# Output projection of a hybrid layer as seven products of block sums through DRAM, with the second norm's transposes set among the up projection's first products

## The chip, the cores and the metric

One core of one Trainium2 chip. The core has engines with a queue each: TensorE (matmul, and its weight load beside it), VectorE, ScalarE, GpSimd, and SyncE, which in this kernel issues all transfers between DRAM and the on-chip memory, one after the other in the order of its queue. An engine takes its instructions in order; one that waits for another engine holds up all that stand behind it.

The metric is the device time of one execution in microseconds, as a median of runs. Beside it there is a hardware profile of one execution, whose span goes from its first to its last instruction.

## The reference

One layer over 1024 tokens of width D = 1024, cut to what matters here (the inner width F of the feed-forward part is 2816):

```python
hx = modulate(rmsnorm(x), sh1, sc1)                  # (T, D)
q, k, v, rq, rk, rv, rg, ga, gb = split(hx @ w_in)
o_na  = neighbourhood_attention(q, k, v, ctx)        # (T, 512)
o_ret = two_way_retention(rq, rk, rv, ctx) * silu(rg)  # (T, 1024)

merged = sigmoid(ga) * (o_na @ w_proj_na) + sigmoid(gb) * (o_ret @ w_proj_ret)
x   = x + g1 * (merged @ w_out)                      # output projection, gated residual
hx2 = modulate(rmsnorm(x), sh2, sc2)                 # second norm
u   = conv3_over_tokens(hx2 @ w_up)                  # (T, 2F), three taps and a bias
a, val = split(u)
x   = x + g2 * ((silu(a) * val) @ w_down)
return rmsnorm(x, final_gain)
```

All inputs and the output are float32.

## The kernel before, in words

**Products.** Each float32 operand is split in a high part (ScalarE copies it to the rounded form, L86) and a low part (VectorE subtracts the copy from the original, L87), and each product is three matmuls: high x high, high x low, low x high. A matmul is 128 x 128 weights against 128 x 512 moving elements. Activations lie in two layouts: channels on the partitions and tokens along the row (128 channels x 512 tokens, a half of the tokens), or tokens on the partitions (a token block is 128 tokens).

**Seven products.** Where the text says "seven products of block sums", a product of 2 x 2 blocks is computed with seven block products in place of eight (the Winograd form): four sums S1 to S4 of the left blocks A11 to A22, four sums T1 to T4 of the right blocks B11 to B22, then A11 B11, S2 T2, A12 B21, S3 T3, S1 T1, A22 T4, S4 B22, whose results are added up. The kernel before does this for the gates, for the up projection (class `Seven`, its subclass `Up`) and for the down projection (`steps`), but not for the output projection. The sums of the down projection's weights (`down_sums`, GpSimd, L1249) are made in three earlier stages and kept in DRAM (`d_w`); its activations' sums go through DRAM too (`d_a`).

**Order.** A scheduler puts the instructions of most stages in the engines' queues by priority and estimated time; what is wrapped in `late(...)`, and the stages under a manual schedule, keep the order of the program. All transfers stand on SyncE's queue.

**The stages around the change.**
- *Merge* (L1588 to L1624, some 87 us): for each of eight blocks `db` of 128 channels and two halves of the tokens, `pret` computes the retention projection in 24 matmuls (`pr`, L110 to L112), VectorE multiplies it by the gate (L1592), GpSimd adds the attention part that waits in DRAM (L1593; VectorE for the last block), and the sum is split into high and low parts that stay on the chip. Blocks run in order 0 to 7. Each block needs two weight tiles (`pret_load`, from `in_w_pret`) and four tiles of gates and attention parts (`merge_load`, from `d_gate` and `d_pn`). Beside them `out_sums` makes the last of the sums for `d_w`, one step per half.
- *Output projection* (`out_proj`, L1631 to L1658, some 95 us): all of `w_out` is on the chip, split. For each of eight token blocks and two halves of D, 24 matmuls (`om`, L121 to L123) give 128 tokens x 512; VectorE multiplies by the gate row `gate1` and adds `x`. The row's mean square goes to ScalarE, then the power of -1/2 to GpSimd.
- *Second norm* (`norm_out`, L1660 to L1692): one token block behind the projection, eight transposes on TensorE (L1671) give channels on the partitions; ScalarE writes the high part with gain and shift (L1677), VectorE the full value (L1679) and the low part (L1680), 128 x 128 each. The values of the first four token blocks go to DRAM (`d_h`); with those of the other four they make the T sums for the up projection's seven products (four VectorE subtractions of 128 x 512 per token block, `d_t`).
- *Up projection, first two column blocks* (`up`, L1701; loop L1838): plain products of 4 x 48 matmuls (24 per branch and half of the tokens), into double banks of PSUM (`u`, 128 x 1024). The first half of both branches of the first block (`early`, L1712) runs between the last projection and the last transposes. After each pair a convolution over the tokens (`conv`, L1754) reads PSUM. Between the pairs `comb` (L1780) loads and splits the T sums, four tiles of 128 x 512 for each of T1 to T4.
- *Up projection, the other 20 column blocks*: units `Up` (L1789, L1848), each seven products of four k-blocks x 3 = 84 matmuls, the weights' sums made by GpSimd (L1380 to L1383).

## Time and profile before

| | |
|---|---|
| device time, median of 3 runs | 1765.64 us (1763.32 to 1767.51) |
| profiled execution, span from first to last instruction | 1759.2 us; what lies around the span is not recorded apart |
| mean granted TensorE clock of the profiled execution | 0.996 |
| TensorE matmul, busy | 1726.0 us (98%), 8405 instructions |
| VectorE, busy | 1284.2 us (73%) |
| ScalarE, busy | 849.2 us (48%) |
| GpSimd, busy | 539.3 us (31%) |
| moved by transfers | 261.10 MB |
| merge stage, 920.5 to 1007.6 | GpSimd busy 29.92 of 87.10 us |

How to read the rows of the profile: a group row has the line of the program, engine, operation, output <- inputs by their names in the program, partitions x elements, the count, then busy time and mean duration of one (ns), then idle time of the engine just before them and what ended it. A row of a stretch (first to last time) has for PE, PEld, DVE (VectorE), ACT (ScalarE) and POOL (GpSimd) the busy time and count, then TensorE's granted clock (1.00 is full), the share of the transfer engines, and GB/s. Rows of waits name the engine that waited, for which tile, and who released it: sum, count and longest. SPq is SyncE's queue. Rows of transfers have the KB of one and the time from issue to landing.

### The profile page before, as it was taken

To read this page: it belongs to the slowest core of one execution; us is meant where nothing else is said; L and a number is where in the kernel's file an instruction comes from. 1 tells how busy PE (TensorE), PEld (TensorE's weight loads), DVE (VectorE), ACT (ScalarE), POOL (GpSimd) and SP (SyncE) were. 2 spreads that over 40 slices of the span, in tenths; PEclk is the share of its full clock that TensorE was granted. 3 is DMA by queue.
4 is the path that set the end of the run, shared out by engine and by line. 5 is a ranking of instruction groups with operands and counts; after the bars stand their busy time and mean duration, and the time that the engine had idled before them with its cause. 6 is when DMAs were issued, how large, how long until landed. Compare 5 with 4: busy or idle time off the path is not lost.

```text
span 1759.2 us, 24801 instructions
## 1 busy us (share of the span) xinstructions
PE 1726.0 (98%) x8405; PEld 1429.3 (81%) x8405; DVE 1284.2 (73%) x2454; ACT 849.2 (48%) x1826; POOL 539.3 (31%) x455
## 2 busy tenths in 40 slices
PE   8999999999999999999999999989999999999997
PEld 4688988888888888778888888778888888788886
DVE  4778887756776766777665557868899889875755
ACT  5666666653443434443444324534444444554444
POOL 1000000003334343555413300165555655211444
PEclk9999999999999999999999999999999999999999
DMA  9143334342231212677557733733322332586754
GB/s 348 61 130 125 95 117 147 117 133 87 73 108 43 72 42 68 203 238 239 200 199 268 246 143 132 254 108 102 108 90 92 118 120 90 170 296 192 239 162 162
DMA packets 139408, 261.10 MB, mean 148 GB/s; under 512 B 15856, under 2 KB 28304, under 8 KB 139280
## 3 DMA queue, kind: packets, MB, share of 16 engines
q1 hardware_dynamic: 139280, 259.51, 44.3%
q8 instruction: 66, 1.08, 0.3%
q14 instruction: 62, 0.51, 0.1%
HBM read 187.34 MB, written 69.48 MB: 146 GB/s over the span
## 4 chain that ended last, share of the span: by engine, by line
PE 43%; issue 6%; DVE 4%; POOL 3%; DMA 1%; ACT 1%; SPq 0%; POOLq 0%; ACTq 0%; DVEq 0%
PE u L1374 30%; PE y L1374 4%; PE pr L112 2%; PE pr L111 2%; PE pr L110 2%; PE om L122 1%; PE om L121 1%; PE om L123 1%; POOL x L1902 1%; DVE wc L87 0%; DVE b L1350 0%; DVE v L1679 0%; POOL pd L1939 0%; DVE hxT L87 0%; POOL x L1947 0%
## 5 line engine op out<-in xcount | busy, mean ns | idle before, releaser
L1374 PE MATMUL u<-T,wc 128*128 128x512 f32 x960 | 227.1, 392 | 5.1 <-ACT pu L1408 5.1
L1374 PEld LDWEIGHTS u<-T,wc 128*128 128x128 f32 x960 | 180.6, 189 | 45.7 <-ACT pu L1408 7.9
L1374 PE MATMUL y<-wc,ahl 128*128 128x512 f32 x924 | 210.6, 389 | 2.7 <-DVE wc L87 1.8
L1374 PEld LDWEIGHTS y<-wc,ahl 128*128 128x128 f32 x924 | 173.3, 188 | 39.7 <-DVE wc L87 2.5
L87 DVE TENSOR_TENSOR wc<-ur,wc 128x512 fp32r<-128x512 f32 x137 | 122.7, 897 | 65.8 <-ACT wc L86 65.8
L86 ACT CAST wc<-ur 128x512 fp32r<-128x512 f32 x137 | 85.0, 621 | 129.7 <-PE y L1374 72.3
L111 PE MATMUL mm<-low,wc 128*128 128x512 f32 (+1 forms) x328 | 124.0, 378 | 0.0
L1374 PE MATMUL u<-h2a,wc 128*128 128x512 f32 x480 | 112.3, 389 | 0.7 <-DVE pu L1417 0.7
L110 PE MATMUL mm<-hx,wc 128*128 128x512 f32 x264 | 107.4, 407 | 0.2 <-ACT wc L589 0.2
L1374 PEld LDWEIGHTS u<-h2a,wc 128*128 128x128 f32 x480 | 90.0, 188 | 19.8 <-DVE pu L1417 1.2
L112 PE MATMUL mm<-hx,wc 128*128 128x512 f32 x264 | 105.2, 399 | 0.0
L86 ACT CAST wc<-s 128x512 fp32r<-128x512 f32 x80 | 49.7, 623 | 93.2 <-PE u L1374 88.3
L123 PE MATMUL mm<-wc,low 128*128 128x512 f32 (+1 forms) x240 | 91.2, 380 | 0.0
L1374 PE MATMUL u<-hxT,wc 128*128 128x512 f32 x384 | 89.6, 389 | 0.0
L1508 POOL TENSOR_TENSOR col<-col,bcol 128x32 f32<-128x32 f32 x1 | 0.3, 253 | 280.7 <-DVE aw L538 280.7
L87 DVE TENSOR_TENSOR wc<-s,wc 128x512 fp32r<-128x512 f32 x80 | 83.5, 1046 | 3.8 <-ACT wc L86 3.4
L1374 PEld LDWEIGHTS u<-hxT,wc 128*128 128x128 f32 x384 | 72.1, 188 | 14.9
L87 DVE TENSOR_TENSOR wc<-raw,wc 128x512 fp32r<-128x512 f32 x92 | 68.0, 746 | 17.7 <-ACT wc L86 17.7
L121 PE MATMUL mm<-wc,hx 128*128 128x512 f32 x192 | 75.2, 392 | 0.6 <-ACT r L1105 0.6
L122 PE MATMUL mm<-wc,hx 128*128 128x512 f32 x192 | 75.2, 392 | 0.0
L1383 POOL TENSOR_TENSOR s<-ur 128x512 f32<-128x512 f32 x20 | 35.7, 1783 | 126.3 <-DVE wc L87 68.7
L86 ACT CAST wc<-raw 128x512 fp32r<-128x512 f32 x92 | 56.8, 621 | 33.0 <-PE pr L112 6.0
(393 smaller groups left out, 4671.3 us busy)
## 6 DMA issues: line engine op xcount, KB each, us to landing
ur<-in_w_up SPq DMA_DIRECT2D x80, 256.0 KB, 2.9
ur<-d_a SPq DMA_DIRECT2D x77, 256.0 KB, 3.1
aw<-in_w_ada SPq DMA_DIRECT2D x32, 512.0 KB, 3.3
pj<-in_w_down SPq DMA_DIRECT2D x44, 256.0 KB, 5.2
d_w<-pj SPq DMA_DIRECT2D x44, 256.0 KB, 2.0
d_a<-sa SPq DMA_DIRECT2D x44, 256.0 KB, 2.0
ur<-d_w SPq DMA_DIRECT2D x44, 256.0 KB, 3.8
d_a<-at SPq DMA_DIRECT2D x33, 256.0 KB, 2.7
```

Source lines behind the costliest of these rows:

```text
L86: act.copy(hi, src)
L87: (lo_eng or vec).tensor_tensor(lo, src, hi.bitcast(F32), ALU.subtract)
L110: pe.matmul(out, wh, xh, start=k == 0, stop=False)
L111: pe.matmul(out, wh, xl, start=False, stop=False)
L112: pe.matmul(out, wl, xh, start=False, stop=k == n - 1)
L121: pe.matmul(out, ah, bh, start=first, stop=False)
L122: pe.matmul(out, ah, bl, start=False, stop=False)
L123: pe.matmul(out, al, bh, start=False, stop=last)
L1374: pe.matmul(out, a, b, start=first and n == 0, stop=last and n == 2, skip_group_check=True)
L1383: pool.tensor_tensor(self.s1, self.a21, self.a22, ALU.add)
L1508: pool.tensor_tensor(col[:, 16:48], col[:, 16:48], bcol[:, 16:48], ALU.add)
L1902: pool.tensor_tensor(z, z, fg[:, gs(dh)], ALU.mult)
```

## The change

- **Output projection as seven products.** Left operands are blocks of the merged activations: A11, A12, A22 are stored by `pret` itself, S1 to S4 are made by VectorE (`mg_sums`, after both blocks j and j + 4 are there), all into `d_m`. Right operands are made by GpSimd (`out_sums`): it multiplies `w_out` by the gate row `gate1` and makes T1 to T4, all into `d_wo`, 3 steps per half of a merge block. Merge blocks run in the order 0, 4, 1, 5, 2, 6, 3, 7. `pret` no longer splits its result. A `Stream` loads the operands from DRAM eight ahead (10 buffers), and `out_ops` splits both per product and k-block.
- **Accumulation.** Products lie in two sets of four PSUM banks, one bank per token block; results are combined on VectorE (`p1`, `u2`, `u3`), and GpSimd adds `x` in half rows. `out_last` finishes a token block's row norm.
- **The norm turned per four token blocks.** `turn2` transposes one channel block of four token blocks into one bank and evicts 128 x 512 at a time; the turns of half 1 stand beside the last product and the first plain up products, those of half 0 beside the next. Plain up products go channel block by channel block over two (column blocks) x two (branches) accumulators. The weights `wu[0]` are loaded and split a second time for the last quarter.
- **T sums** are made by GpSimd per channel block (`token_sums`), in place of VectorE per token block; `d_h` is gone.
- **PSUM** of the up projection is eight single banks; the first two column blocks are copied to `uu` by ScalarE ahead of their convolution.
- **`w_down` sums** are all made before the merge stage: one step in two of the gates stage in place of one in three.

The core of the diff:

```diff
-    RET_SUMS, GATE_SUMS = 5, 9
+    RET_SUMS = 5
...
-        if n % 3 == 1:
+        if n % 2:
             next(gate_sums, None)
...
+    def out_sums():
...
+        for j in range(KH):
+            nxt = []
+            for n, (t, c) in enumerate(zip(ts, ("B11", None, "B21", "B22"))):
+                late(pool.tensor_tensor(t, t, gate1[:, n % 2 * 512 : n % 2 * 512 + 512], ALU.mult))
+                if c:
+                    sync.dma_start(d_wo[j, BLOCKS[c]], t)
+                if j + 1 < KH:
+                    nxt.append(load(j + 1, n))
+                yield
+            b11, b12, b21, b22 = ts
+            t1, t2, t4 = (tile_() for _ in range(3))
+            for c, o, x, y in (("T1", t1, b12, b11), ("T3", b12, b22, b12), ("T2", t2, b22, t1), ("T4", t4, b21, t2)):
+                late(pool.tensor_tensor(o, x, y, ALU.subtract))
+                sync.dma_start(d_wo[j, BLOCKS[c]], o)
+                yield
+            ts = nxt
...
     def pret(db, half):
...
-        g = sg[db, 1, half]
+        mg[db, half] = g = sg[db, 1, half]
         vec.tensor_tensor(g, m, g, ALU.mult)
         (vec if db == KB - 1 else pool).tensor_tensor(g, g, sg[db, 0, half], ALU.add)
-        h_, l_ = gtile(half, F32R, "mh"), gtile(half, F32R, "ml")
-        split(h_, l_, g)
-        mg[db, half] = (h_, l_)
+        if (db // KH, half) != (0, 1):
+            sync.dma_start(d_m[{(0, 0): A11, (1, 0): A12, (1, 1): A22}[db // KH, half], db % KH], g)
+
+    def mg_sums(j):
+        a11, a21, a12, a22 = (mg[j + KH * i, half] for i in range(2) for half in range(2))
+        s1, s2, s3, s4 = (gtile(n % 2, F32, "s") for n in range(4))
+        for c, o, x, y, op_ in ((S1, s1, a21, a22, ALU.add), (S2, s2, s1, a11, ALU.subtract), (S3, s3, a11, a21, ALU.subtract), (S4, s4, a12, s2, ALU.subtract)):
+            vec.tensor_tensor(o, x, y, op_)
+            sync.dma_start(d_m[c, j], o)
...
+    dbs = [db for j in range(KH) for db in (j, j + KH)]
...
+    mg_sums(0)
+    ostream = Stream([(j, c) for p in ORDER for j in range(KH) for c in p], 8, out_source, xr_load)
-    for db in range(2, KB):
+    for n, db in enumerate(dbs[2:]):
         wp[db] = pret_load(db)
         merge_load(db)
-        if db == 2:
-            brow(0, gate1)
         for half in range(2):
             pret(db, half)
-            next(out_sums, None)
+            for _ in range(3):
+                next(out_sums, None)
+        if db >= KH:
+            mg_sums(db - KH)
+    for _ in out_sums:
+        pass
...
+    def out_ops(p, js):
+        tl = []
+        for j in js:
+            a, w = (gtile(1, F32R, "ah"), gtile(1, F32R, "al")), wtile()
+            split(*a, ostream.get((j, ORDER[p][0])))
+            split(w[:, 0], w[:, 1], ostream.get((j, ORDER[p][1])))
+            tl.append((j, a, w))
+        return tl
...
+    def out_last(tb, dh, p, x):
+        z[tb, dh] = t = t_tile("z")
+        vec.tensor_tensor(t, bank(p % 2, tb % QB), x, ALU.add)
+        out_square(tb, dh)
+        s = ss[:, tb]
+        pool.tensor_scalar(s[:, 3:4], s[:, dh : dh + 1], 1.0 / D, s[:, 2:3], ALU.mult, ALU.add)
+        pool.tensor_tensor(s[:, 4:5], s[:, 3:4], mhalf[:, 0:1], ALU.pow)
+        for d in (1 - dh, dh):
+            xn[tb, d] = t_tile("xn")
+            act.activation(xn[tb, d], z[tb, d], AF.Copy, scale=s[:, 4:5])
...
+    def turn2(half, kb, tp):
...
+        for b in range(QB):
+            pe.transpose(tp[:, b * P : (b + 1) * P], xn[half * QB + b, kb // KH][:, kb % KH * P : (kb % KH + 1) * P], ident)
...
+        act.activation(h_, tp, AF.Identity, bias=sh, scale=a)
+        v2[half, kb] = v = t_tile("v")
+        vec.tensor_scalar(v, tp, a, sh, ALU.mult, ALU.add)
+        vec.tensor_tensor(l_, v, h_.bitcast(F32), ALU.subtract)
+
+    def token_sums(k):
+        b11, b21, b12, b22 = v2[0, k], v2[0, k + KH], v2[1, k], v2[1, k + KH]
+        for c, o, x, y in ((0, b11, b12, b11), (2, b12, b22, b12), (1, b22, b22, b11), (3, b21, b21, b22)):
+            pool.tensor_tensor(o, x, y, ALU.subtract)
+            sync.dma_start(d_t[c, k], o)
...
+    out_steps(0, True, False)
+    for b in range(QB):
+        p1[b] = t_tile("p1")
+        act.copy(p1[b], bank(0, b))
...
+    out_steps(5, False, True, 2)
+    tl = out_ops(5, (2, 3))
+    t7 = out_ops(6, (0, 1))
+    for b in range(QB):
+        out_mm(5, b, tl, False, True)
+        if b == 1:
+            t7 += out_ops(6, (2, 3))
+        out_last(QB + b, 0, 5, p1[b])
+
+    for n in range(2):
+        for b in range(QB):
+            out_mm(6, b, t7[n : n + 1], False, True)
+    tl = t7[2:]
+    for b in range(QB):
+        turn2(1, KORD[b], bank(1, 2 + b % 2))
+        out_mm(6, b, tl, False, True)
+        out_last(b, 1, 6, u2[b])
...
+    for n, k in enumerate(KORD):
+        if n + QB < KB:
+            turn2(1, KORD[n + QB], bank(1, 2 + n % 2))
+        for br in range(2):
+            up_k(us4[br], wu[0][br], 1, k, n)
+    for n, k in enumerate(KORD):
+        turn2(0, k, bank(0, n % 2))
+        if k >= KH:
+            token_sums(k - KH)
+        for br in range(2):
+            up_k(us4[2 + br], wu[1][br], 1, k, n)
+    for n, k in enumerate(KORD):
+        for br in range(2):
+            up_k(us4[2 + br], wu[1][br], 0, k, n)
+    wu[0] = [up_load(seq[1], br) for br in range(2)]
+    for n, k in enumerate(KORD):
+        for br in range(2):
+            up_k(us4[br], wu[0][br], 0, k, n)
...
-    for n, j in enumerate(seq[:PLAIN]):
-        us2 = []
-        for br in range(2):
-            u, wu = (u_tile(2 * n + br), up_load(j, br)) if n else early[br]
-            for half in range(2) if n else (1,):
-                up(u, wu, half)
-            us2.append(u)
+    for n in range(PLAIN):
         for c in ((1, 0), (2, 3))[n]:
             combs[f"T{c + 1}"] = comb(c)
-        conv(j, *us2)
+        uu = [tap.tile([P, T], F32, tag="uu", bufs=4, name="uu") for _ in range(2)]
+        for br in range(2):
+            for half in range(2):
+                act.copy(uu[br][:, half * 512 : half * 512 + 512], us4[2 - 2 * n + br][half])
+        conv(seq[n], *uu)
```

## The prediction

> **What bounds the kernel now.** I read the page first, then the busy time by stretch, the waits of TensorE and of the DMA queue, and last the rows of the stage that changes.

> ```profile
> span 1759.2 us, 24801 instructions
> PE 1726.0 (98%) x8405; PEld 1429.3 (81%) x8405; DVE 1284.2 (73%) x2454; ACT 849.2 (48%) x1826; POOL 539.3 (31%) x455
> ```
> ```profile
> 920.50:1007.60 87.10, 87.10 (x386) 72.13 (x385) 46.34 (x67) 35.16 (x60) 29.92 (x22) 1.00 0.76 258
> 1007.60:1102.30 94.70, 94.70 (x445) 78.60 (x444) 62.08 (x155) 31.82 (x70) 3.83 (x7) 1.00 0.40 148
> ```
> ```profile
> L110 PE MATMUL pr<-orr,wc x128: 389/389/389, 920.8 to 1007.2; 128*128 128x512 f32 x128
> L112 PE MATMUL pr<-orr,wc x128: 389/389/389, 921.3 to 1007.6; 128*128 128x512 f32 x128
> ```

> TensorE is busy 98% of the span, and in the two stretches that change (merge products to 1007.6, output projection to 1102.3) all of the time, at clock 1.00. So each matmul taken out is a gain at its pitch, each new wait of TensorE a loss in full. The pitch is not the 389 ns of a record: 384 matmuls start between 920.8 and 1007.6, so 0.2266 us each.

> ```profile
> PE u L1374 <- ACT pu L1408: 5.1, 1, 5.1
> PE tpn L1366 <- DVE ona L1369: 3.3, 1, 3.3
> PE u L111 <- DVE h2l L1680: 0.6, 2, 0.3
> ```
> ```profile
> 719.80:723.00 3.20, 3.17 (x12) 2.87 (x13) 3.20 (x6) 3.15 (x7) 3.20 (x4) 0.50 0.68 250
> 1156.50:1160.00 3.50, 3.43 (x8) 2.75 (x9) 3.50 (x5) 0.53 (x2) 0.74 (x1) 0.52 0.56 148
> ```

> The only waits near the change are 5.1 us, in the first seven-product unit of the up projection, and 0.6. The first two rows show a second price: after each of these waits (they end at 719.8 and 1156.5) the granted clock is 0.50 and 0.52 for 3.2 to 3.5 us. A wait of 3.3 us or more thus costs some 1.6 us on top.

> **The gain.** Seven products of 4 k-blocks by 4 token blocks by 3 passes are 336 matmuls in place of 384. 48 x 0.2266 = 10.9 us. The 64 transposes and the 192 plain up matmuls stay. Splits (ScalarE cast, VectorE remainder) go from 32 to 56, evictions grow to 128x512: both engines are under 70% busy here, so this costs nothing by itself. What decides is the order of the queues, which I took from the changed kernel as built: each engine takes its instructions in that order, and SyncE issues every DMA.

> **First wait: weights of merge block 3.** The merge products run over blocks 0, 4, 1, 5, 2, 6, 3, 7, two halves of 24 matmuls (5.44 us) each. The two weight loads of block 3 stand on SyncE behind the stores of block 6's sums:

> ```
> d_wo<-T1, d_wo<-T3, d_wo<-T2   of w_out block 2   [each waits GpSimd]
> d_m<-S1, d_m<-S2, d_m<-S3, d_m<-S4   of merge blocks 2, 6   [wait VectorE]
> raw<-in_w_pret, raw<-in_w_pret   for merge block 3
> ```

> S1 needs the last product of block 6, and TensorE has nothing to run between block 6 and block 3. In the kernel before these loads stood ahead of all such stores. That SyncE really stands still for such a store is seen here:

> ```profile
> 996.90 1.30 POOL L1249 TENSOR_TENSOR pj<-pj 128x512 f32<-128x512 f32 x1
> ```
> ```profile
> 998.23 0.33 SPq L1257 DMA_DIRECT2D d_w<-pj  x1
> 998.61 0.43 SPq L1571 DMA_DIRECT2D sg<-d_pn  x1
> ...
> SPq L1251 <- POOL pj L1249: 17.3, 7, 4.6
> ```

> The sum ends at 998.2, the store goes out at 998.23, and the load behind it only then; seven such stores held the queue 17.3 us, which hid behind loads made earlier. Prices:

> ```profile
> L1593 POOL TENSOR_TENSOR sg<-sg x14: 1277/1294/1674, 929.1 to 1000.7; 128x512 f32<-128x512 f32 x14
> ...
> L1249 POOL TENSOR_TENSOR pj<-pj x8: 1282/1292/1302, 956.1 to 996.9; 128x512 f32<-128x512 f32 x8
> ```
> ```profile
> L1592 DVE TENSOR_TENSOR sg<-pr,sg 128x512 f32<-128x512 f32 x15 | 10.3, 686 | 5.5 <-PE pr L112 5.0 <-ACT sg L1575 0.5
> L87 DVE TENSOR_TENSOR wc<-raw,wc 128x512 fp32r<-128x512 f32 x16 | 11.2, 703 | 2.8 <-ACT wc L86 2.8
> L86 ACT CAST wc<-raw 128x512 fp32r<-128x512 f32 x16 | 9.7, 620 | 9.3 <-PE pr L112 6.0 <-DMA raw<-in_w_pret 1.7 <-PE u L1374 1.4
> L1575 ACT ACTIVATE sg<-sg 128x512 f32<-128x512 f32 x8 | 5.1, 632 | 10.0 <-DMA sg<-d_gate 10.0
> ```
> ```profile
> raw<-in_w_pret SPq DMA_DIRECT2D x16, 256.0 KB, 3.5
> sg<-d_gate SPq DMA_DIRECT2D x16, 256.0 KB, 4.0
> ur<-d_t SPq DMA_DIRECT2D x16, 256.0 KB, 4.9
> d_t<-vo SPq DMA_DIRECT2D x8, 256.0 KB, 2.0
> ...
> 943.53 1.66 POOL L1593 TENSOR_TENSOR sg<-sg 128x512 f32<-128x512 f32 x1 [3.23 <-DVE sg L1592]
> ```

> Least case, GpSimd otherwise idle: block 6 ends at 12 x 5.44 = 65.3 (counted from 920.8). Product 0.69, sum on GpSimd 1.29, three w_out sums queued behind it 3.9, four stores of 0.33 each 1.3, load 2.9 to 3.5, cast 0.62: TensorE goes on at 76, a wait of 11. But GpSimd is not idle. Its queue holds, from the add of block 1 to those three sums, 8 merge adds and 23 w_out operations: 31 x 1.29 = 40 us. The fourth add ended at 945.2, that is 24.4. The four VectorE sums behind it and a split (5 x 0.69) end at 27.8; their stores head the gate loads of block 1, which land 4 us later, then sigmoid 0.63 and product 0.69: that add starts at 33. The gate loads of block 2 stand behind a w_out store in the same way, and GpSimd waits about 6 us for them. 33 + 40 + 6 = 79; stores, load and cast 5.4: TensorE starts block 3 near 85, a wait of 20. With the contended 1.67 in place of 1.29 it passes 25; I bound it at 11 and 23, since VectorE is idle while TensorE waits.

> [...]

> **Second wait: first output product.** Its third matmul needs the low part of A11, which stands on VectorE behind, for merge block 7: product, add, a split for product two, three sums, another split, the fourth sum. With its own subtraction 9 x 0.69 = 6.2 after the last merge matmul, less two matmuls 0.45: 5.7 at least (5.3 with 0.65 each). The splits ahead also wait for loads that SyncE issues after the last w_out store. I take 7, and 9 at most.

> **Inside the seven products** I charge nothing: operands are fetched eight ahead, and a product of 48 matmuls (10.9) covers eight casts (5.0) and eight subtractions with four evictions (8.3). Without that cover each product would cost the difference, and with GpSimd alongside VectorE it is thin.

> **Third: the turn.** Products five and six end in a row norm of four token blocks, then transposes that need all four.

> ```profile
> L1897 ACT ACTIVATE xr<-z 128x512 f32<-128x512 f32 x8 | 5.0, 628 | 14.9 <-DVE z L1972 8.9 <-POOL z L1958 6.0
> L1897 ACT ACTIVATION_READ_ACCUMULATOR xr<-z 128x1 f32 x8 | 1.5, 186 | 0.0
> L1906 POOL TENSOR_SCALAR ssf<-ssf 128x1 f32<-128x1 f32 x8 | 3.0, 381 | 16.3 <-ACT xr L1897 16.3
> L1907 POOL TENSOR_TENSOR ssf<-ssf,mhalf 128x1 f32<-128x1 f32 x8 | 4.7, 586 | 0.5
> L1909 ACT ACTIVATE x<-x,ssf 128x512 f32<-128x512 f32 x8 | 5.7, 717 | 5.6 <-POOL ssf L1907 5.6
> ```

> A token block takes ScalarE 0.63 + 0.19, then GpSimd 0.38 + 0.59 while ScalarE waits or casts a weight (0.62), then two scaled copies, 1.4: up to 3.4 us, four of them 13.7, against 9.5 of matmuls that TensorE has until then. Later the up matmuls wait several times under 2 us on VectorE, which evicts, scales and subtracts. I take 4; nothing, if casts and norms interleave better, to 8.

> **Fourth: T operands before weights.** The weights of the second value block of the up projection (wu[0], br 1) are cast on ScalarE behind the four casts of one T operand, and these need all sixteen token sums on GpSimd (16 x 1.29 = 20.6; 22.9 at 1.43), a store 2.0 partly beside, and the last d_t load. TensorE has six steps of 1.76 (six matmuls, four transposes), 47 matmuls and 3 more, 21.9, from about 1 us after the first sum starts. Sums end at 21 from there, issue 1.3, load 3 to 4.9, two casts 1.2: 27. Wait 5; between 0 and 9.

> **Fifth: copies before the first unit.** The plain up products now lie in eight single banks. For the second pair ScalarE makes four copies out of PSUM and two activations before it casts the first seven-product unit's weight; VectorE does four convolution steps before its low part.

> ```profile
> L1819 ACT COPY uu<-u 128x512 f32<-128x512 f32 x20 | 11.8, 588 | 3.1 <-PE u L1374 1.9
> L1759 ACT ACTIVATE ta<-uu,cb,cw 128x1024 f32<-128x1024 f32 x20 | 24.9, 1246 | 10.3 <-DVE uu L1398 9.9
> ...
> L1760 DVE SCALAR_TENSOR_TENSOR ta<-u,cw,ta 128x1023 f32<-128x1023 f32 x2 | 2.6, 1278 | 1.4 <-ACT ta L1759 1.4
> L1763 DVE TENSOR_TENSOR at<-ta,at 128x1024 f32<-128x1024 f32 x2 | 2.4, 1214 | 0.0
> ```

> 4 x 0.59 + 1.25 = 3.6, four steps of 1.28, 0.69, a product 1.21 and 0.69: 11.3, of which TensorE works 2.7. At least 8.5 against the 5.1 that stands there now: +3.4. As the T casts come late too, I take +5, up to 9.

> The gate stage gets eight more GpSimd sums (8 x 1.29) and their DMAs on SyncE; GpSimd was 40 to 55% busy there on the page, so I charge nothing.

> **Sum.** -10.9 + 20 + 7 + 4 + 5 + 5 = +30.1. Three of the waits are new ones over 3.3 us (first, second, fourth): 3 x 1.6 = 4.8. Together +34.9. Against the profiled span 1759.2 that is 1794. The median of the runs shown, 1765.64, is 6.4 above the span, and I keep that distance: 1800.5, rounded to 1800. The smallest price of each (11, 5.3, 0, 0, 3, clock 3.2) gives +11.6, 1777; the largest (23, 9, 8, 9, 9, clock 6.4) gives +53.5, 1819.

> **Rivals.**
> *Faster: the loads win.* If block 3's weights and A11 land before TensorE needs them, and the 5.1 us wait goes as well, the time is 1765.6 - 10.9 - 5.1 = 1749.6, 1750. It decides where SyncE reaches those two loads before 980 of the old trace, 6 us before block 3's turn. For it: stores held SyncE 17.3 us before and TensorE never waited. Against: a store ahead of the loads needs a product of block 6 itself. 7%.
> *Only the least chains bind.* GpSimd keeps up, and each wait is at its floor: the 1777 above, 1774 without its clock term. Against it are 31 operations behind an add that cannot start before 33. 20%.
> *The waits just eat the gain,* two of them missing: 1766. 4%.
> *GpSimd is the bound throughout.* With VectorE beside it at 1.67 (the slow records of the merge adds), first and fourth wait grow by 12 and 6: 1818, and with the fifth at its 9 as well 1822. 14%.
> *That the change does not do what it says* I rule out for the count: 336 products stand in the built order.
> The forecast holds 55%.

> A measurement of this kernel tells about 0.2% (3.5 us) from no change. Faster 0.07, same 0.04, slower 0.89. Range 1774 to 1822: the first and third rival lie below it, and little above.

> **What would show it.** In the profile after: a wait of TensorE of 11 us or more at the merge product that starts block 3, released by the cast of its weight, with SyncE issuing that load just after stores of d_wo and d_m; a second of 6 to 9 us at the first output product, released by VectorE; output products otherwise without a gap, 336 of them; GpSimd above 60% busy in the merge stage against 34% now; waits at the last plain up products and at the first unit; clock near 0.5 after each long one. I am wrong if block 3's weights are fetched ahead, if TensorE's waits between 920 and 1180 sum to less than 16 us, or if the seven products themselves starve, which I priced at nothing.

## The result, and the profile after

The changed kernel takes 1826.51 us (median of 4 runs, 1825.42 to 1828.57), the kernel before 1765.49 us beside it (1763.32 to 1767.51): a ratio of 1.035, 95% interval 1.0335 to 1.0365. The forecast was slower by 34.5 us (1800, range 1774 to 1822); it is slower by 61.0. The sign and the places of the waits held, the size did not.

The page's head, and TensorE's waits by what they waited for and who released them (sum, count, longest):

```profile
span 1823.6 us, 25072 instructions
PE 1731.4 (95%) x8357; PEld 1430.1 (78%) x8357; DVE 1314.0 (72%) x2362; ACT 865.0 (47%) x1850; POOL 634.8 (35%) x531
```
```profile
PE pr L111 <- ACT wc L87: 28.6, 1, 28.6
PE u L1734 <- ACT ah L87: 9.3, 1, 9.3
PE u L1734 <- ACT wc L87: 7.4, 3, 5.4
PE u L1778 <- ACT xn L1767: 6.3, 7, 3.2
PE u L122 <- ACT wc L87: 6.1, 1, 6.1
...
PE u L1734 <- DVE pu L1412: 2.6, 1, 2.6
PE u L1734 <- DVE wc L88: 2.6, 1, 2.6
...
PE u L1778 <- DVE v L1784: 1.5, 1, 1.5
```

The span grew by 64.4 us, from 1759.2 to 1823.6, and TensorE's share fell from 98% to 95%. The first five rows are the five places that the prediction named, in another order: the weights of merge block 3 (28.6), the first output product (9.3), the first units (7.4, with 2.6 and 2.6 below), the turn (6.3 and 1.5), the reloaded weights of branch 1 (6.1). Two stretches, the merge and the output products up to the first turn:

```profile
922.10:1040.60 118.50, 89.94 (x385) 73.77 (x384) 43.99 (x53) 19.76 (x32) 60.84 (x46) 0.87 0.79 277
1050.20:1127.60 77.40, 74.36 (x314) 60.45 (x314) 57.11 (x75) 42.05 (x84) 23.47 (x26) 0.96 0.76 260
```

GpSimd went from 34% to 51% of the merge stage, not over 60% as forecast; transfers stand at 79% and 76% of their engines' time, against 76% and 40% before.

**How the first wait came about.** SyncE's queue, then VectorE, GpSimd, ScalarE and TensorE, in order of time (start, duration; in brackets idle time before and its releaser):

```profile
998.17 0.32 SPq L1632 DMA_DIRECT2D d_wo<-pj  x1
999.02 0.45 SPq L1572 DMA_DIRECT2D sg<-d_pn  x1
999.51 0.43 SPq L1574 DMA_DIRECT2D sg<-d_gate  x1
...
1002.91 0.69 DVE L1651 TENSOR_TENSOR sg<-pr,sg 128x512 f32<-128x512 f32 x1 [11.40 <-DMA sg<-d_gate]
...
1003.73 1.26 POOL L1652 TENSOR_TENSOR sg<-sg 128x512 f32<-128x512 f32 x1 [0.71 <-DVE sg L1651]
1004.95 4.60 POOL L1639 TENSOR_TENSOR pj<-pj 128x512 f32<-128x512 f32 x3
...
1006.24 3.65 SPq L1640 DMA_DIRECT2D d_wo<-pj  x3
1009.99 1.97 SPq L1661 DMA_DIRECT2D d_m<-s  x4
1012.05 1.29 SPq L92 DMA_DIRECT2D raw<-in_w_pret  x2
...
1015.47 0.62 ACT L87 CAST wc<-raw 128x512 fp32r<-128x512 f32 x1 [25.96 <-DMA raw<-in_w_pret]
...
1016.14 0.79 PE L111 MATMUL pr<-orr,wc 128*128 128x512 f32 x1 [28.55 <-ACT wc L87]
```

The last merge product before the wait ended at 987.6. The gates that it is multiplied by were only asked for at 999.0, behind a store of `d_wo` whose sum GpSimd finished at 998.1. So VectorE multiplied at 1002.9 after 11.4 us idle, and GpSimd added at 1003.7. GpSimd's next three sums of `w_out` ended at 1009.6; their stores held SyncE until 1009.9, the merge sums were stored from 1010.0, and behind those stores, at 1012.05, stands the load of block 3's weights. It lands, is cast at 1015.47, and TensorE goes on at 1016.1.

**The clock.** The stretches in which the granted clock was low, or just after:

```profile
991.30:1016.10 24.80, 0.00 (x0) 0.00 (x0) 6.66 (x6) 0.62 (x1) 17.30 (x14) 0.50 0.75 270
1016.10:1021.90 5.80, 5.76 (x14) 4.46 (x15) 1.58 (x3) 2.69 (x5) 0.00 (x0) 0.50 0.98 349
1021.90:1027.00 5.10, 5.10 (x24) 4.22 (x23) 2.48 (x4) 1.06 (x2) 1.57 (x2) 0.99 0.64 244
1050.20:1055.90 5.70, 5.47 (x12) 3.92 (x13) 5.01 (x9) 3.10 (x6) 0.00 (x0) 0.50 0.94 302
1127.60:1131.00 3.40, 2.90 (x8) 2.21 (x9) 0.69 (x1) 2.87 (x6) 0.82 (x2) 0.53 0.69 191
1185.80:1192.50 6.70, 3.93 (x9) 3.03 (x10) 5.65 (x9) 5.97 (x12) 0.00 (x0) 0.50 1.02 339
1206.20:1219.80 13.60, 8.87 (x18) 5.65 (x19) 13.60 (x8) 3.94 (x7) 12.76 (x7) 0.51 0.16 59
1226.80:1230.10 3.30, 2.78 (x7) 2.21 (x8) 2.14 (x3) 0.00 (x0) 0.99 (x1) 0.50 0.45 112
```

Behind the wait of 28.6 the clock stays at 0.50 for 5.8 us (to 1021.9), behind that of 9.3 for 5.7, and at the units, where three short waits follow one of 5.4, for 13.6 us, of which TensorE is busy 8.9. Busy time at half clock sums to 5.76 + 5.47 + 2.90 + 3.93 + 8.87 + 2.78 = 29.7 us, about half of it lost (the records of merge matmuls go from 0.39 to 0.79 us there): 14.9. Before it was 1.7 in these stages.

The clock of this trace changes on a raster. Read in windows of 0.5 us, it drops at 991.3, 1045.9, 1127.8, 1185.9, 1206.3 and 1226.8 and comes back at 1022.0, 1056.1, 1131.2, 1192.7, 1220.0 and 1230.2, and all these times lie whole multiples of 3.41 us apart. So each slow stretch of this trace lasts a whole number of steps, its idle time included (9, 3, 1, 2, 4 and 1). Of the step in which the wait of 28.6 ends 2.5 us are work, and the clock stayed low for the next step too; of the step in which the turn's wait of 3.2 ends 3.1 us are work, and the clock came back at its end. In the row of short waits at the units it took four steps. Three waits end 0.9 (those of 28.6 and 9.3) and 2.7 us (the one before 1188.6) into a step: 5.8, 5.7 and 4.1 us of slow work follow, to the end of the next step. Two end 0.3 (the turn's) and 0.5 us (the one before 1227.3) into a step: 3.1 and 2.9 follow, to the end of the same step. In this trace, then, the price of a wait went with where in a step it ended; no run varies that place alone.

### The profile page after: what moved, and what is told of

Same layout as the page of the kernel before. It is cut to its first block, busy times and chain, and to the rows that moved or that the text cites. A ratio compares the mean times of both kernels' runs of the same rounds, so it can differ in the third digit from the quotient of the medians.

```text
span 1823.6 us, 25072 instructions
## 1 busy us (share of the span) xinstructions
PE 1731.4 (95%) x8357; PEld 1430.1 (78%) x8357; DVE 1314.0 (72%) x2362; ACT 865.0 (47%) x1850; POOL 634.8 (35%) x531
## 5 line engine op out<-in xcount | busy, mean ns | idle before, releaser
L87 ACT CAST wc<-ur 128x512 fp32r<-128x512 f32 x137 | 85.0, 622 | 117.2 <-PE y L1734 71.2
L1734 PE MATMUL u<-h2a,wc 128*128 128x512 f32 x480 | 116.0, 397 | 8.7 <-ACT wc L87 6.1
L112 PE MATMUL mm<-low,wc 128*128 128x512 f32 (+1 forms) x328 | 124.0, 378 | 0.0
L111 PE MATMUL mm<-hx,wc 128*128 128x512 f32 x264 | 107.4, 407 | 0.2 <-ACT wc L590 0.2
L87 ACT CAST wc<-s 128x512 fp32r<-128x512 f32 x80 | 49.7, 622 | 95.4 <-PE u L1734 92.4
L87 ACT CAST wc<-raw 128x512 fp32r<-128x512 f32 x92 | 56.6, 620 | 70.9 <-DMA raw<-in_w_pret 39.9
L88 DVE TENSOR_TENSOR wc<-s,wc 128x512 fp32r<-128x512 f32 x80 | 87.2, 1092 | 1.3 <-ACT wc L87 0.9
L1734 PE MATMUL u<-wc,ah 128*128 128x512 f32 x224 | 72.0, 404 | 9.3 <-ACT ah L87 9.3
L111 PE MATMUL pr<-orr,wc 128*128 128x512 f32 x128 | 51.2, 400 | 28.6 <-ACT wc L87 28.6
L122 PE MATMUL mm<-wc,hx 128*128 128x512 f32 x192 | 75.2, 392 | 0.6 <-ACT r L1106 0.6
## 6 DMA issues: line engine op xcount, KB each, us to landing
ur<-in_w_up SPq DMA_DIRECT2D x80, 256.0 KB, 2.8
ur<-d_a SPq DMA_DIRECT2D x77, 256.0 KB, 3.4
pj<-in_w_down SPq DMA_DIRECT2D x44, 256.0 KB, 4.7
d_w<-pj SPq DMA_DIRECT2D x44, 256.0 KB, 2.0
d_a<-sa SPq DMA_DIRECT2D x44, 256.0 KB, 2.0
ur<-d_w SPq DMA_DIRECT2D x44, 256.0 KB, 3.4
d_a<-at SPq DMA_DIRECT2D x33, 256.0 KB, 2.5
```

Of the source, the lines that this page charges most:

```text
L87: act.copy(hi, src)
L88: (lo_eng or vec).tensor_tensor(lo, src, hi.bitcast(F32), ALU.subtract)
L111: pe.matmul(out, wh, xh, start=k == 0, stop=False)
L112: pe.matmul(out, wh, xl, start=False, stop=False)
L122: pe.matmul(out, ah, bh, start=first, stop=False)
L1734: pe.matmul(out, a, b, start=first and n == 0, stop=last and n == 2, skip_group_check=True)
```

## The experiments

Line numbers in rows of an experiment are those of its own program, some 5 to 20 lines on. Three rounds of questions: whether the queue or the engines make the first wait, whether the other waits are independent, and what holds the stretch behind the second norm.

### The first wait

**e1_hoist**: each merge block's weights and gates are asked for one block earlier.

```diff
+    ahead(dbs[2])
     for n, db in enumerate(dbs[2:]):
-        wp[db] = pret_load(db)
-        merge_load(db)
+        if n + 3 < KB:
+            ahead(dbs[n + 3])
```

> Weights and gates of each merge block are asked for one block earlier; nothing else changes. Theory of the queue (SyncE stands at the stores of block 6's sums with block 3's weights behind them): the wait of 28.6 us at block 3 falls below 4, TensorE's waits between the merge stage and the first output product sum to less than 18 (37.9 now), most of it at the first output product, and the time is 1792 to 1800. Rival (GpSimd with its 32 sums, or the transfers at 80% share, are the bound and the queue only shows it): the wait moves to block 7 or to the first output product, the sum stays at 28 or more and the time above 1812.

Measured 1813.07 us (2 runs). The merge stage still waits 8.7 + 2.8, the first output product 8.8:

```profile
PE u L1739 <- ACT ah L87: 8.8, 1, 8.8
PE pr L111 <- ACT wc L87: 8.7, 2, 8.5
...
PE pr L113 <- DVE wc L88: 2.8, 3, 1.6
```

The waits sum to 20.3, between the two expectations (18 and 28), and the time is on the rival's side. An earlier block's weights (issued at 983.3, TensorE goes on at 988.0) now stood behind merge sums and `d_wo` stores in the same way. Not decided by this run.

**e2_nosums**: GpSimd's work on w_out left out; the kernel leaves out the sums, so its output is not the reference's.

```diff
-        return d_wo[j, BLOCKS[c]] if c in BLOCKS else d_m[ROWS[c], j]
+        if c in BLOCKS: return io["w_out"][...]
...
-    out_sums = out_sums()
+    out_sums = iter(())
```

> GpSimd's scaling and sums of w_out are left out with their loads and stores (32 operations, 28 stores); the operands T and B of the output products are loaded from w_out as it is, so the output projection's values are not the reference's. The loads of block 3's weights still stand behind the stores of the merge sums. Theory of the queue: the wait at block 3 stays, at its floor of 9 to 12 us (product 0.69, add 1.29, four sums, four stores 0.33 each, load 3, cast 0.62), and the time is 1798 to 1806. Rival (GpSimd is the bound): without its work the wait is under 3 and the time 1793 or less.

Measured 1790.87 us (2 runs), the rival's number; no wait of TensorE in the merge stage at all. But the expectation's premise was wrong: without the sums the scheduler also put block 3's weights ahead of the merge sums' stores, so the run takes away work, stores and order at once, and cannot tell them apart.

**e5_lag6**: e1_hoist, and each store of the stage is issued six stores later. GpSimd's sums, the transfers and their sizes are unchanged.

```diff
+    def put(dst, t, lag=6):
+        pend.append((dst, t))
+        while len(pend) > lag:
+            sync.dma_start(*pend.pop(0))
...
-                sync.dma_start(d_wo[j, BLOCKS[c]], o)
+                put(d_wo[j, BLOCKS[c]], o)
```

> The earlier loads of e1_hoist, and each store of the merge stage is issued six stores later, so that its data are ready when SyncE reaches it. Same work on every engine, same transfers. Theory (what is left of the wait in e1_hoist, 11.5 us in the merge stage, is SyncE standing at stores that are not ready): TensorE's waits in the merge stage fall below 4 us and the time is 1798 to 1806, the wait at the first output product staying near 9. Rival (GpSimd or the transfers cannot deliver faster): the waits of the merge stage and the first output product together stay above 17 us and the time is 1810 or more.

Measured 1802.15 us (2 runs):

```profile
PE u L1747 <- ACT wc L87: 18.9, 4, 11.6
...
PE pr L113 <- DVE wc L88: 2.1, 1, 2.1
```
```profile
915.00:1030.00 115.00, 101.13 (x438) 82.46 (x437) 60.05 (x71) 25.62 (x43) 62.94 (x46) 0.95 0.92 324
```

With the same 46 GpSimd operations and transfers at 92% of their engines' time in the stage, the 28.6 us are 2.1 + 0.2. This settles it: the first wait was the order of SyncE's queue, loads behind stores whose data were not ready, and not what GpSimd or the transfers can deliver. The first output product now waits 11.6 (the longest of the four in the first row), since the operands' loads (from 1022.2) stand behind the last merge sums' delayed stores (1020.0); it cost 2.3 us of what was won.

### Are the waits independent?

**e3_a11**: the first product's left operands in tiles of the later norm.

```diff
-            a, w = (gtile(1, F32R, "ah"), gtile(1, F32R, "al")), wtile()
+            a, w = tuple(h2[0][j][:, i] for i in range(2)) if p == 0 else (gtile(1, F32R, "ah"), gtile(1, F32R, "al")), wtile()
```

> Only the first output product's left operands are written to other tiles (those of the later norm, free until then), so that their casts stand ahead of the casts of T2 on ScalarE. Theory (A11's cast stands behind the casts of T2, which wait for the last stores of w_out's sums): the wait of 9.3 at the first output product falls to 1 to 3 us and the time to 1814 to 1819. Rival (the operands from DRAM come too late whatever the order): as long a wait stands there or at the second product, and the time is 1823 to 1828.

Measured 1824.74 us (2 runs; the first wait was 30.9 in the profiled one). TensorE's waits, then VectorE's in the output products:

```profile
PE u L1778 <- DVE z L1760: 5.0, 1, 5.0
...
PE u L1734 <- DVE h2a L88: 1.3, 1, 1.3
```
```profile
DVE al L88 <- ACT ah L87: 14.0, 5, 6.7
```
```profile
1088.00:1108.00 20.00, 19.60 (x86) 15.79 (x85) 13.11 (x15) 8.55 (x17) 12.34 (x10) 1.00 0.96 317
```

The place was right: the wait of 9.3 is 1.3. But 5.0 of it came back at the turn, where none had been for `z`: VectorE stood 14.0 us for casts of later left operands (changed kernel: 5.2; with the casts of the right operands it is 20.9 against 14.8), with the transfers at 96% of their engines' time in this stretch (changed kernel: 84%). The rival holds by the time, though not by the place that it named: the wait came back at the turn, 76 us later, not at the first or second product.

**e4_brmajor**: the last quarter of the plain up products branch by branch.

```diff
-    for n, k in enumerate(KORD):
-        for br in range(2):
+    for br in range(2):
+        for n, k in enumerate(KORD):
             up_k(us4[br], wu[0][br], 0, k, n)
```

> Only the last quarter of the plain up products is reordered: all of branch 0, then all of branch 1, so 24 matmuls (5.4 us) stand between the release of the weight tile and the first use of branch 1's. Theory (branch 1's weights are cast too late, behind the casts of the T operands): the wait of 6.1 goes and the time is 1817 to 1820. Rival (the T operands themselves are late, so that whatever TensorE gains is lost again at the first unit of seven products): the waits from there on grow by as much and the time is 1823 to 1828.

Measured 1831.13 us (2 runs), 4.6 more than the changed kernel and 3 above the rival's range. Of the 4.6, 3.1 stand ahead of the merge stage in the traced executions (its first product starts at 925.3, in the changed kernel at 922.1), where the edit changes nothing.

```profile
PE u L1734 <- ACT wc L87: 13.4, 3, 11.5
...
PE u L122 <- ACT wc L87: 1.4, 1, 1.4
```

The wait of 6.1 is 1.4, and that at the first unit grew from 5.4 to 11.5. The rival holds: what TensorE is spared here it waits some 18 us later, at the first unit.

**e12_tokv**: T sums on VectorE again (`vec` for `pool` in `token_sums`).

> The changed kernel with one thing undone: the sixteen T sums are made by VectorE again, as in the kernel before, not by GpSimd. Theory (GpSimd's 24 us of T sums, 1.29 to 1.5 each, slow VectorE beside it and end when VectorE has been idle for 10 us; everything behind is queued up): the sums end some 6 us earlier, the waits from 1180 on (6.1, 5.4, 1.3, 0.7, 2.6, 2.6) shrink from 18.7 to 10 or less and the time is 1814 to 1819. Rival (ScalarE's 24 us of casts, copies and activations behind the sums are the bound): TensorE waits as long and the time is 1822 to 1827.

Measured 1823.62 us (2 runs). The wait of 6.1 is gone, the first unit waits 10.9 (in the row below, the longest):

```profile
PE u L1734 <- ACT wc L87: 13.0, 3, 10.9
```

The waits behind 1180 are 17.9 us against 18.7. The rival holds: that GpSimd makes the T sums cost nothing that was not covered by what comes after them.

**e6_post**: e4_brmajor, and the first unit's three first products ahead of the second pair's copies and convolution and of T3 and T4, in banks that are free early.

```diff
-    us4 = [[u_tile() for _ in range(2)] for _ in range(4)]
+    us4 = [...]; us4 = us4[2:] + us4[:2]
...
         conv(seq[n], *uu)
+        if n == 0:
+            for i, k in todo[:3]:
+                units[i].step(k)
```

> Merge stage and output products as in the changed kernel; behind them the last quarter of the plain up products by branch, and the first unit's three first products (with banks that are free early) ahead of the casts of T3 and T4 and of the second pair's copies and convolution on ScalarE and VectorE. Theory (the waits from 1180 on, 18.7 us with the branch 1 weights' and 19.7 in e4_brmajor, are ScalarE's and VectorE's queue: some 24 us of work between the last token sum and the first unit's weights): they fall below 9 and the time is 1811 to 1817. Rival (the T operands' way over GpSimd, DRAM and back is the bound): they stay above 15 and the time is 1822 or more.

Measured 1820.02 us (2 runs): waits behind 1180 of 1.2, 0.8, 6.3 and 3.7, 12.0 in all, between the two expectations.

**e7_all**: e5_lag6, e3_a11 and e6_post together.

> The edits of e5_lag6, e3_a11 and e6_post together, on the changed kernel; same sums, products and transfers. Theory (each of the waits is an order of queues, and they are independent): the new waits that stay are those of the turn (8 us) and some 8 more, the clock's loss is 6, so 1755 + 8 + 8 + 6 = 1777, between 1770 and 1788: by and large the kernel before. Rival (the transfers, 280 to 330 GB/s from 1050 to 1110, and VectorE beside GpSimd are the bound of the stretch): waits come back at the turn or at the last plain products, and the time is 1792 or more.

Measured 1794.07 us (4 runs): in the rival's range, though not for its reason. The largest wait, 10.0, stood at the first output product, and SyncE and ScalarE show why:

```profile
1020.06 2.49 SPq L1702 DMA_DIRECT2D d_m<-s  x4
1022.61 0.45 SPq L1582 DMA_DIRECT2D r<-d_m  x1
...
1025.98 0.62 ACT L87 CAST h2a<-r 128x512 fp32r<-128x512 f32 x1 [23.21 <-DMA r<-d_m]
```

The operands' first load is issued right behind the stores of the last merge sums: again an order.

**e8_ask**, e7_all with `ostream.ask(6)` ahead of the last merge block:

> e7_all, and the first six operand loads of the output products are asked for before the last merge block, so that they stand ahead of the stores of its sums on SyncE. Theory (in e7_all the first operand load is issued at 1022.6, behind the last sums' stores, and TensorE waits 10.0 for it): the wait falls below 2 and with the clock's loss behind it the time is 1781 to 1786. Rival (transfers and VectorE bound the seven products, and an earlier start only waits later, as in e3_a11): the turn's waits grow by as much and the time is 1790 or more.

Measured 1787.33 us (2 runs). The wait of 10.0 became 1.0, 2.6 and 0.8 within the first two products, and the turn's first waits grew from 0.7 to 2.1: two thirds won, the rest given back.

**e9_units**, e7_all with the first unit's products ahead of the first convolution too; **e10_turn**, e7_all with the turns of half 1 two token blocks later; **e11_best**, all edits.

> e7_all, and the first unit's three first products stand ahead of the first pair's convolution too (VectorE's four convolution steps, 2.29 us each beside GpSimd). Theory (VectorE's queue holds the first unit's low parts behind those steps): the waits of 6.4 and 3.7 at the units fall to less than 5 together and the time is 1785 to 1790. Rival (the T operands by way of DRAM bind): they stay above 8 and the time is 1792 or more.

> e7_all, and the turns of half 1 start two token blocks of the last product later, so that 12 more matmuls (2.7 us) stand ahead of the first. Theory (the chain VectorE, ScalarE, GpSimd, ScalarE of the fourth token block's norm is 3 us longer than what TensorE has): the waits of 0.7 and 3.2 at the first turns go, the later ones (0.9, 1.2, 1.5) stay or shrink, and the time is 1788 to 1792. Rival (ScalarE's queue is the bound, so that the later turns and the first up products wait for it instead): no change, 1793 or more.

> All edits of e7_all to e10_turn together. Theory (independent orders of queues): 1794 less 11, 6 and 4 is 1773, between 1765 and 1779. It beats the kernel before only if nothing new waits. Rival (a bound of VectorE, ScalarE or the transfers under the queues): 1783 or more.

Measured 1793.33 (2 runs), 1792.60 (2 runs) and 1784.08 us (4 runs; ratio to the kernel before 1.0112, interval 1.0095 to 1.0128). In e9_units the waits 6.4 and 3.7 became 1.2, 7.3 and 3.2, one product later. In e10_turn 0.7 and 3.2 became 1.9 and 2.7. Neither gained anything that can be told: e9_units ends on its rival's side, e10_turn between its two expectations. e11_best, on its rival's side, is e8_ask less 3.

### What holds the stretch behind the second norm

**e13_bestv** (e11_best, T sums and one of the two scaled row copies on VectorE) and **e14_bestv2** (the same on e8_ask):

> e11_best with the T sums by VectorE, and of the two scaled copies of a finished row one by VectorE (both by ScalarE until now). Theory: waits of 7.4 and 3.2 at the units fall by 6 or more, those of the turn (3.0, 3.0) by 3, and the time is 1770 to 1776. If nothing new waits it comes down to 1765; below 1762 it would beat the kernel before. Rival (the same total of work on ScalarE and VectorE per microsecond binds): 1782 or more.

> e8_ask with the two moves to VectorE of e13_bestv, but without the earlier start of the first unit and the later turn of e11_best. Theory (those two edits gained nothing by themselves): within 3 us of e13_bestv, 1770 to 1778. Rival: 1782 or more.

Measured 1784.89 and 1782.88 us (4 runs each), the rival's side in both by the time. The traces show more than the times. The turn's waits fell from 10.8 us in e8_ask to 6.3 in e14_bestv2, and from the first merge product to the end e14_bestv2 takes 853.5 us, e8_ask 859.6. But that product starts at 927.7 in the traced execution of e14_bestv2 and at 924.5 in that of e8_ask, ahead of the stages that the edits touch: half of the 6 us that the moves won there is hidden by a slower beginning. The waits at the units did stay.

**e15_noconv** and **e16_defer**: e14_bestv2 without VectorE's convolution steps for the first two column blocks (which leaves out their neighbour taps), and e14_bestv2 with the first block's convolution behind the first unit's three first products and the second block's behind five more (`units[i].step(k)` for `todo[:3]` and `todo[3:8]` ahead of `conv`). So e16_defer moves two things, where its expectation names one.

> e14_bestv2, with the eight convolution steps of VectorE (1.28 us each, up to 2.3 beside GpSimd) left out for the first two column blocks, so that two column blocks have no neighbour taps and their values are not the reference's; all else stands. Theory (both column blocks end together in the changed order, and the lump of VectorE's work behind them, two convolutions and the splits of the T operands, is the bound there): the waits from 1160 on (2.8, 2.9, 0.9, 3.7) fall below 4 together, and with the clock's loss the time is 1771 to 1777. Rival (ScalarE's casts, copies and activations bind): they stay above 8 and the time is 1780 or more.

> e14_bestv2, with the second column block's convolution put behind five more products of the units, nothing left out. Theory of the lump: the waits from 1160 on fall by half and the time is 1774 to 1779. Rival (VectorE's total is too large for the stretch, or ScalarE binds): 1781 or more.

Measured 1771.46 us (5 runs) and 1777.71 us (4 runs; ratio 1.0068, interval 1.0041 to 1.0094), both times in the theory's range. The waits fell less than the theory said: from the first unit on (1162.1, 1158.8 and 1159.9 in the traces) they sum to 11.0 us in e14_bestv2, to 6.1 in e15_noconv (3.2 and 2.9; below 4 expected) and to 9.2 in e16_defer (half expected). Stretches of e14_bestv2, then of e15_noconv:

```profile
1160.00:1180.00 20.00, 13.81 (x46) 9.76 (x44) 19.54 (x20) 15.21 (x24) 10.01 (x6) 0.83 0.56 186
1180.00:1200.00 20.00, 15.10 (x55) 11.12 (x54) 20.00 (x16) 6.82 (x12) 16.95 (x10) 0.83 0.38 132
```
```profile
1160.00:1180.00 20.00, 17.02 (x62) 12.57 (x61) 17.09 (x19) 13.46 (x24) 12.22 (x8) 0.86 0.52 174
1180.00:1200.00 20.00, 20.00 (x90) 16.54 (x89) 19.04 (x19) 7.59 (x11) 13.94 (x9) 1.00 0.41 130
```

In e14_bestv2 VectorE is busy 39.5 of these 40 us and TensorE 28.9; without eight of VectorE's steps TensorE is busy 37.0, VectorE still 36.1. By the medians, taking the steps away is worth 11.4 us and e16_defer 5.2. Not all of that is the edit: from the first merge product to the end the traced executions take 853.5, 847.0 (e15_noconv) and 849.7 us (e16_defer), so 6.5 and 3.8; the rest lies ahead of the merge stage. In the kernel before, the first column block ends 96 plain matmuls (21.8 us) ahead of the second; in the changed order both get their second half last, 48 matmuls (10.9 us) apart, and two convolutions and sixteen T splits fall due there. So in e14_bestv2 VectorE's work behind the second norm costs TensorE time, and ScalarE's, which e15_noconv leaves as it is, does not explain it. How much is the amount of that work and how much its place, the two runs do not separate.

For e4_brmajor and e12_tokv the traces show another engine. Until the first unit's weight is cast, ScalarE is busy 16.7 of 16.8 us in e4_brmajor (1193.1 to 1209.9) and 17.7 of 17.9 in e12_tokv (1183.9 to 1201.8), and that cast stands last in the row. In e4_brmajor VectorE had stood idle for 10.0 us just before, for T operands that were still on their way through DRAM. There ScalarE's queue behind the late T operands held TensorE, as the rival of e12_tokv had it; once the order was changed (e14_bestv2), VectorE's work did.

e16_defer is the fastest version with the reference's values, 49 us under the changed kernel and 12 above the one before. No version beat the one before. What the last 12 us are made of was not settled: its largest waits are single ones of 1 to 2.7 us from the merge stage to the units, with the granted clock between 0.83 and 1.00 in stretches of 20 us from 1080 to 1200.

## Why the prediction was right or wrong

| step | forecast, us | measured, us |
|---|---|---|
| 48 matmuls less | -10.9 | -10.9 by count (224 + 112 output matmuls) |
| first wait | 20 | 28.6 |
| second wait | 7 | 9.3 |
| third, the turn | 4 | 6.3 + 1.5 = 7.8 |
| fourth | 5 | 6.1 |
| fifth, over what stood there | 5 | 7.4 + 2.6 + 2.6 - 5.1 - 0.7 = 6.8 |
| clock | 4.8 | 14.9 - 1.7 = 13.2 |
| sum | 34.9 | 60.9 of the span's 64.4 |

Of the 3.5 us that the sum leaves open, 1.3 stand ahead of the merge stage, which begins at 922.1 in place of 920.8; the rest is not placed. The distance from span to median, kept at 6.4, is 2.9 for the changed kernel, which brings 64.4 down to 61.0. Each execution on record took 1.7 to 2.2 us more than its own span; most of the 6.4 was a profiled execution that was faster than the median of its kernel. Keeping it was an error that by luck took 3.5 us off the miss.

Every wait stands where it was forecast, and every one was priced too low. Two terms are most of the miss.

**The clock** (8.4 of it) is the step that failed outright. It took 3.3 us of slow work, 1.6 lost, after each of three long waits. Both places from which this was read ran slow for 3.4 us (719.6 to 723.0 and 1156.5 to 1159.9 in the kernel before), one step of the raster, and none of the six above is shorter. Measured are 5.8 and 5.7 us behind the long waits, which end 0.9 us into a step, and six slow stretches in place of three: 13.6 us at the units alone, which were given no clock at all. Part of this is chance: the turn's wait of 3.2 us is followed by 3.1 us of work at half clock here, and by 5.6 in e1_hoist, where the matmuls stand 0.43 us apart in place of 0.23 until 1119.9.

**The first wait** (8.6) had the right chain and one step of it too short: "GpSimd waits about 6 us" for gate loads that stand behind a store. GpSimd's row of block 1's add starts at 957.99, 35.9 after the stage's begin (33 forecast), and the last sum ends at 1009.55: 51.6 us, of which 40.6 is work (40 forecast) and 11.0 idle. Most of that is one idle of 8.4, for block 2's gates (asked for at 982.2, behind stores of merge sums). Later start, longer idle: 87.4 after the stage's begin, not 79; stores, load and cast behind it took 6.6, not 5.4. GpSimd's own speed, where the upper bound was sought, was right.

**VectorE's prices** were those of an undisturbed VectorE. Its merge sums and its convolution steps, beside GpSimd and alone, in the changed kernel:

```profile
L1660 DVE TENSOR_TENSOR s<-sg 128x512 f32<-128x512 f32 x4 | 6.9, 1754 | 2.9 <-POOL sg L1652 2.9
L1660 DVE TENSOR_TENSOR s<-sg,s 128x512 f32<-128x512 f32 x2 | 1.4, 692 | 0.1
```
```profile
L1901 DVE SCALAR_TENSOR_TENSOR ta<-uu,cw,ta 128x1023 f32<-128x1023 f32 x1 | 2.3, 2293 | 0.0
```
```profile
L1901 DVE SCALAR_TENSOR_TENSOR at<-uu,cw,at 128x1023 f32<-128x1023 f32 x1 | 1.3, 1278 | 0.0
```

0.69 becomes 1.75, 1.28 becomes 2.29. The fifth wait's four convolution steps (9.2 us for the second pair, 5.1 forecast) were priced at the undisturbed 1.28; of that wait, 2.6 us are released by a low part that stands behind them, 7.4 by ScalarE. GpSimd's sixteen T sums, too, took 24.2 us, with VectorE at work beside them until 1173.3 (20.6 to 22.9 forecast).

**The second wait** was forecast as released by VectorE; it was ScalarE, whose casts of A11 stood behind casts of T2 that wait for the last `d_wo` loads (the prediction named those loads as an aside). e3_a11 confirms the place. "Inside the seven products I charge nothing" held in the changed kernel, but with less margin than was thought: e3_a11 shows that an earlier start is spent there.

**The turn** was on the forecast chain and cost 7.8 in place of 4. ScalarE's two row copies have a part in it (the moves of e14_bestv2 took 4.5 us off the turn's waits of e8_ask); a later start (e10_turn) gained nothing, and the rest was not taken apart.

**The fourth and fifth** were priced as separate waits. e4_brmajor and e12_tokv show that they are one: taking away the fourth gives it to the fifth (6.1 and 5.4 become 1.4 and 11.5, and 0 and 10.9). How these 11 to 13 us were divided between the two was of no consequence.

Of the rivals, "GpSimd is the bound throughout" came nearest by its number (1818 to 1822) and is refuted by its mechanism (e5_lag6). The range failed at the top since its upper bounds of the first wait (23) and of the clock (6.4) were set from the same two short terms.

## What to carry to other kernels

Here a store to DRAM on SyncE's queue, which issues everything in order, was a wait for its producer, and the loads behind it inherited that wait (28.6 us of TensorE's at block 3): put loads a block ahead of such stores and the stores a few behind their data (24 us in e5_lag6) before asking whether the engines are fast enough. Before a wait is priced as a gain, look at what the engine that releases it has queued next: the waits taken away in e3_a11, e4_brmajor, e12_tokv and e9_units came back, whole or in good part, at the next place where the same queues were late. A matmul saved is worth its pitch (0.23 us here) only if nothing else falls due at the same time; count what each engine must do in the microseconds between the end of one phase and the first need of the next.

## What the runs showed of the hardware

VectorE's merge sums (128 x 512 float32) took 2.5 times as long beside GpSimd (0.69 to 1.75 us), its convolution steps from `uu` 1.8 times (1.28 to 2.29). Its gate products, with one input in PSUM, kept 0.69 beside GpSimd (at 960.4, 989.5 and 990.8). GpSimd can be the slow one, too: its first weight sum of the units took 6.35 us, a later one 1.29 (at 1243.7), while VectorE's T splits beside it kept their 0.6 us each:

```profile
1199.66 6.35 POOL L1384 TENSOR_TENSOR s<-ur 128x512 f32<-128x512 f32 x1 [17.16 <-PE u L124]
```

The same sum took 5.42 us in the kernel before, also beside T splits (six in 3.69 us), and 1.30 in e7_all, where VectorE stood idle for most of it; no run isolates the cause.
